# Zero products between the first transposes, other places for key transposes, query copies and weight splits in a two-layer trunk kernel

## The chip, the cores and the metric

The kernel runs on one core of a Trainium2 chip. A core has these engines: TensorE (PE, matrix products; PEld loads its stationary operand), VectorE (DVE), ScalarE (ACT), GpSimd (POOL), and SyncE (SP), on whose queue nearly all the transfers of this kernel stand. Each engine goes through its own instructions in the order in which the program issued them and waits on semaphores for the others. The metric is the time of one execution in microseconds (us); lower is better.

## What is computed

One inference step of a diffusion trunk: two layers over 1024 latent tokens (with 128 cached context keys) and 128 prompt tokens, model width 1024, all in float32. Cut to what matters here:

```python
for layer in range(2):
    mod = silu(c) @ w_mod[layer] + b_mod[layer]             # shift, scale, gate
    h = rms_norm(x, g_pre) * (1 + scale) + shift
    if layer == 0:                                           # A: attention, B: pooling
        q, k, v, ga, ub, gb = split(h @ w_in_e)
        q, k = axial_rope(rms_norm(q, q_norm)), axial_rope(rms_norm(k, k_norm))
        o_a = softmax(q @ [ctx_k, k].T / 8) @ [ctx_v, v]     # 8 heads on 2 key heads
        o_b = multiscale_pool(ub, b_map, b_scale)
        y = concat(o_a * silu(ga), o_b * silu(gb)) @ w_out_e
    else:                                                    # C: neighbourhood, D: latent attention
        y = concat(o_c * silu(gc), o_d * silu(gd)) @ w_out_o
    x = x + gate * rms_norm(y, g_post)
```

## The kernel before

Tokens lie in nine row tiles of 128 (eight latent, one prompt), the model width in eight slices k of 128. A float32 product is made of three: each operand is split into a high part, rounded to a type that PE takes at full rate, and a low part, the rest. So `hTh`/`hTl`, `whi`/`wlo`, `QP`, `KH`/`KL` are high and low halves: a high part is a cast, mostly on ACT, a low part a subtraction on DVE or POOL. `kn.vtt` is a two-operand instruction on DVE, `kn.ptt` the same on POOL, `kn.acopy` a copy or cast on ACT, `kn.tr` a transpose on PE through the identity.

The program is a list of stages. Within one, `weave(main, fill)` issues the main steps (products of PE) in order and puts the steps of `fill` between them by cost: every entry is (cost, function), and a fill step is issued when the costs before it have kept pace with those of the main list. `merge(a, b, off)` mixes two fill lists evenly. An entry whose function does nothing only spends cost, that is, pushes the next ones back. So the order on every engine is fixed when the program is built; an engine never goes past an instruction that waits.

What the change touches:

- **First stage** (lines 581 to 670): row tiles of x are loaded, normed and transposed in groups of three. `norm_x(t)` squares a tile with a row sum on ACT, takes the root and its reciprocal, and scales on DVE. `mod_block` makes the shift and scale columns that the norm of a slice needs; `pn(k, g)` transposes slice k of group g (`tp`), applies scale and shift (`hf`), casts `hTh` on ACT and makes `hTl` on POOL. `kvg` adds the products of key and value weights. `zeros(n)` issues n products of a zero tile into the same accumulators, which add nothing.
- **Query stage** (lines 803 to 814): `q_main(0)` and `q_main(1)` make the queries of four heads each. After every pair of row tiles `q_evac` norms and rotates it: a square on ACT, `hss`, `q` and the products `t` on DVE, `t` and `Q` on POOL. The keys come in the same way in pieces: `kv1` norms, `kv2` rotates (`t<-k,rtk` on DVE, `k` on POOL, `kp` for the prompt), and `kv3` transposes (`kT` on PE) and splits into `KH` (ACT) and `KL` (DVE). The argument 0 and 1 is the key tile of four row tiles each, 2 the prompt's. `wl` and `gs` are streams of weight chunks, `_load` issues the transfer, `need` the split.
- **Gate stage** (lines 925 to 942): twelve chunks `ch_main(0)` to `ch_main(11)` of gates and pooling input. In the last ones stand `units[0].prep` (the queries transposed and split, see below) and `maxima` of unit 0, with `rows` after the end of the stage.
- **Units 0 to 7**: attention of two heads and 512 queries each. `maxima` finds a row bound (`mp` products on PE, `mx` on DVE), `scores` makes `st` on PE and `P` on ACT, POOL adds the P of nine key tiles into `acc`, and `fin` divides the finished unit before: `divide` takes four reciprocals `srow` on DVE and then multiplies `oT` by `srow`. `split_heads` copies the transposed queries out of PSUM into `QP` (high part in its head's half, low part in the other) and `QM`.
- **Side work of the units**: `wo.split1(i, veng)` splits a slice of the output weights, the low part on DVE if the second argument is true, else on POOL.
- **Out projection of layer 0 and first chunks of layer 1** (lines 1364 to 1373): the stream `st` of layer 1's weight chunks; `fills[7]` and `fills[8]` are the fill lists of the last two row tiles. `H.make` norms the new x for layer 1 (`hf`, `hT1h`, and `hT1l` on POOL), `cg` are the first products of layer 1.
- **Latent attention of layer 1** (line 2260): `L.split_uk(1)`, one split of the key weights, in the side list of the units.

## Time and profile before

| | |
|---|---|
| median of three runs | 1590.68 us (1585.31 to 1592.05) |
| profiled execution, its own time | 1590.44 us |
| its span in the trace | 1588.6 us (1.84 us lie outside) |
| PE busy | 1517.0 us, 95% of the span |
| DVE, ACT, POOL busy | 803.0, 654.9, 613.6 us |

The stages lie in the span as follows: first stage and key and value projection to about 70 us, query stage to 142, gate stage to 320, units 0 to 7 to 540, out projection to 652, then layer 1 with the neighbourhood attention, the latent attention and its out projection.

A row of a timeline gives start, length, engine, line, operation and its tiles, the number of instructions that it joins, and in brackets how long the engine sat idle before it and which engine's work ended that. A matmul row shows 0.28 us for one product at full clock although they start 0.12 us apart: they are pipelined. [...]

### The profile page before, as it was taken

How to read it: one execution, taken by the hardware profiler on the slowest of the kernel's cores; microseconds unless marked ns; L12 is line 12 of the kernel's file. 1: busy time of each engine (PE TensorE's matmuls, PEld its weight loads, DVE VectorE, ACT ScalarE, POOL GpSimd, SP SyncE). 2: the span in 40 equal slices, each digit the busy share in tenths (PEclk: the TensorE clock that was granted, in tenths of full speed). 3: DMA queues.
4: the chain of work that ended last, by engine and by line, in shares of the span. 5: the costliest groups of instructions: out<-in, count | busy, mean ns of one | idle time of the engine just before them, and what ended most of it. 6: DMA issues, size and time to landing. Idle time of an engine off the chain costs nothing.

```text
span 1588.6 us, 23314 instructions
## 1 busy us (share of the span) xinstructions
PE 1517.0 (95%) x8927; PEld 1234.9 (78%) x8927; DVE 803.0 (51%) x1788; ACT 654.9 (41%) x1402; POOL 613.6 (39%) x508
## 2 busy tenths in 40 slices
PE   7989999989999999899999999999999999999998
PEld 5977999955555588798999999999976666665786
DVE  4574332347667655534354443424574545545643
ACT  4332222155554432435444544444454434445311
POOL 1643122057668423750312203101256656565221
PEclk8999999989999999999999999999999989999999
DMA  9334113130000222230403131131000000013241
GB/s 346 91 132 137 56 34 110 39 123 22 0 14 29 78 87 95 71 60 14 91 23 76 39 75 26 35 111 47 1 19 20 15 27 15 21 50 114 94 147 53
DMA packets 114078, 104.78 MB, mean 66 GB/s; under 512 B 41776, under 2 KB 99952, under 8 KB 113968
## 3 DMA queue, kind: packets, MB, share of 16 engines
q1 hardware_dynamic: 113792, 103.23, 21.6%
q8 instruction: 70, 1.15, 0.3%
q14 instruction: 40, 0.33, 0.1%
q10 hardware_dynamic: 176, 0.07, 0.0%
HBM read 87.54 MB, written 15.75 MB: 65 GB/s over the span
## 4 chain that ended last, share of the span: by engine, by line
PE 80%; DVE 8%; ACT 6%; POOL 3%; issue 2%; DMA 1%; SPq 0%; ACTq 0%; DVEq 0%; POOLq 0%
PE cg L115 15%; PE yps L115 11%; PE st L115 10%; PE gate L115 8%; PE pv L115 8%; PE lat L115 4%; PE mp L115 4%; PE cpv L115 3%; PE cS L115 2%; PE cT L124 2%; PE dq L115 2%; DVE mx L968 2%; PE qkv L115 1%; PE kv L115 1%; PE modps L115 1%
## 5 line engine op out<-in xcount | busy, mean ns | idle before, releaser
L968 DVE TENSOR_REDUCE mx<-mp 128x1 f32<-128x384 f32 x384 | 189.5, 547 | 99.9 <-PE mp L115 98.5
L142 POOL TENSOR_TENSOR acc<-acc,P 128x1024 f32<-128x1024 f32 x84 | 201.6, 2400 | 69.0 <-ACT P L1008 66.0
L1008 ACT ACTIVATE P<-st 128x512 f32<-128x512 f32 x256 | 148.4, 598 | 157.9 <-PE st L115 147.4
L115 PE MATMUL yps<-whi,ohl 128*128 128x512 f32 x576 | 182.8, 393 | 0.0
L115 PE MATMUL cg<-hT1h,whi 128*128 128x384 f32 x480 | 169.7, 353 | 1.8 <-DVE hf L151 1.2
L142 POOL TENSOR_TENSOR wlo<-raw,whi 128x1024 fp32r<-128x1024 f32 x30 | 72.0, 2401 | 247.5 <-ACT whi L131 172.3
L115 PE MATMUL cg<-hT1h,wlo 128*128 128x384 f32 x480 | 162.5, 339 | 1.9 <-POOL wlo L142 1.9
L115 PE MATMUL cg<-hT1l,whi 128*128 128x384 f32 x480 | 162.1, 338 | 0.0
L115 PEld LDWEIGHTS yps<-whi,ohl 128*128 128x128 f32 x576 | 108.1, 188 | 25.8 <-issue 3.7
L115 PE MATMUL yps<-wlo,ohl 128*128 128x512 f32 x288 | 112.1, 389 | 0.0
L115 PE MATMUL gate<-hTh,whi 128*128 128x384 f32 x288 | 99.2, 345 | 4.9 <-ACT whi L131 4.9
L115 PE MATMUL gate<-hTh,wlo 128*128 128x384 f32 x288 | 98.3, 341 | 0.3 <-DVE wlo L139 0.3
L115 PE MATMUL gate<-hTl,whi 128*128 128x384 f32 x288 | 97.8, 340 | 0.0
L115 PEld LDWEIGHTS cg<-hT1h,whi 128*128 128x128 f32 x480 | 90.7, 189 | 6.6 <-issue 3.3
L1616 ACT ACTIVATE cs<-cs,cnm 128x640 f32<-128x640 f32 (+1 forms) x64 | 54.8, 857 | 91.7 <-DVE cnm L149 91.1
L115 PEld LDWEIGHTS cg<-hT1h,wlo 128*128 128x128 f32 x480 | 90.6, 189 | 2.2 <-POOL wlo L142 2.2
L115 PEld LDWEIGHTS cg<-hT1l,whi 128*128 128x128 f32 x480 | 90.9, 189 | 0.5
L115 PE MATMUL pv<-P,dV 128*64 128x512 f32 x288 | 72.8, 633 | 1.7 <-DVE mx L968 1.7
L131 ACT CAST whi<-raw 128x1024 fp32r<-128x1024 f32 (+2 forms) x60 | 61.9, 1036 | 27.2 <-DMA raw<-in_w_in_e 12.8
L115 PE MATMUL mp<-KH,QP 128*128 128x384 f32 x192 | 61.3, 382 | 9.6 <-DVE QP L139 4.2
L139 DVE TENSOR_TENSOR wlo<-raw,whi 128x1024 fp32r<-128x1024 f32 (+2 forms) x30 | 38.4, 1288 | 61.4 <-ACT whi L131 56.0
L115 PE MATMUL st<-QH,dKh 96*128 96x512 f32 x144 | 63.5, 441 | 2.2 <-ACT P L1008 2.2
(424 smaller groups left out, 3563.8 us busy)
## 6 DMA issues: line engine op xcount, KB each, us to landing
raw<-in_w_in_o SPq DMA_DIRECT2D x20, 512.0 KB, 4.1
raw<-in_w_in_e SPq DMA_DIRECT2D x18, 512.0 KB, 7.5
wmb<-in_w_mod SPq DMA_DIRECT2D x16, 512.0 KB, 8.3
wm<-in_w_mod SPq DMA_DIRECT2D x16, 512.0 KB, 7.3
wg<-in_w_mod SPq DMA_DIRECT2D x16, 512.0 KB, 4.7
x<-xr SPq DMA_DIRECT2D x9, 512.0 KB, 4.8
xr<-x SPq DMA_DIRECT2D x9, 512.0 KB, 4.6
xn<-in_x_sample SPq DMA_DIRECT2D x8, 512.0 KB, 7.1
```

Source lines behind the costliest of these rows:

```text
L115: self.nc.tensor.matmul(out=out, lhsT=l, rhs=r, start=st, stop=sp)
L124: self.nc.tensor.transpose(out, in_, self.ident[0:n, 0:n])
L131: self.nc.scalar.copy(out=out, in_=in_)
L139: self.nc.vector.tensor_tensor(out=out, in0=a, in1=b, op=op)
L142: self.nc.gpsimd.tensor_tensor(out=out, in0=a, in1=b, op=op)
L968: kn.nc.vector.tensor_reduce(out=self.mx[:, h, t, c:c + 1], in_=b, axis=AX.X, op=ALU.max)
L1008: kn.nc.scalar.activation(out=P[:, h], in_=a, func=AF.Exp, scale=self.scale)
L1616: nc.scalar.activation(out=s[:, 0:n], in_=s[:, 0:n], func=AF.Exp, bias=nm, accum_out=sm)
```

## The change

1. First stage: `norm_x` of tiles 3 to 5 is split. The squares of tiles 3 and 4 (`norm_x1`) stand ahead of the first `pn`, that of tile 5 behind it; roots and scaling (`norm_x2`) follow. The six first transposes go in pairs with five zero products between; four stand before the mod block, ten instead of three behind it, and three each before, between and behind the next two `pn`. `kvg` issues its nine products by operand rather than by row tile.
2. Query stage: `kv3(0)` moves from `q_main(0)` to `q_main(1)`; there the order is `kv2(2)`, `kv2(1)`, `kv3(0)`, `kv3(2)`, `kv3(1)`, all ahead of the last six fill steps.
3. Gate stage: `units[0].prep` is in chunk 9, ten maxima pieces in chunk 10, the rest and the rows in chunk 11.
4. Units: the multiplication in `divide` is on POOL for five units; `split_heads` makes the low part before `QM`, and copies `QM` from `QP` in SBUF.
5. Weight splits: slice 5 of the output weights and the first four chunks of layer 1 have their low part on DVE; chunk 2 of the latter is loaded earlier and split in `fills[8]`; `split_uk(1)` is one slot earlier.

```diff
+    rx = {}
+    def norm_x1(t):
+        ss = rx[t] = kn.T([128, 1], tag="xss3", bufs=3)
+        nc.scalar.activation(out=kn.T([128, 1024], tag="sqx", bufs=1), in_=xn[t], func=AF.Square, accum_out=ss)
+    def norm_x2(t):
+        kn.vts(xn[t], xn[t], kn.rstd(rx[t], D, [128, 1], "x"))
...
     def kvg(k, ts):
-        for t in ts:
-            c = slice(128 * t, 128 * t + 128)
-            o = kvps(t)
-            kn.mm(o, hTh[k][:, c], kv.hi(k), False, False)
-            kn.mm(o, hTh[k][:, c], kv.lo(k), False, False)
-            kn.mm(o, hTl[k][:, c], kv.hi(k), False, k == 7 and (t == 8 or t % 2 == 1))
+        for i in range(3):
+            for t in ts:
+                c = slice(128 * t, 128 * t + 128)
+                last = i == 2 and k == 7 and (t == 8 or t % 2 == 1)
+                kn.mm(kvps(t), (hTl if i == 2 else hTh)[k][:, c], (kv.lo if i == 1 else kv.hi)(k), False, last)
...
     zeros(5, True, False)
-    tps = [kn.prenorm_t(k, xn[0:3]) for k in range(2)]
+    tps = [kn.B("tp") for k in range(2)]
+    for i in range(3):
+        for k in range(2):
+            kn.tr(tps[k][:, 128 * i:128 * i + 128], xn[i][:, 128 * k:128 * k + 128])
+        if i < 2:
+            zeros(5, False, False)
+    zeros(4, False, False)
     m = kn.mod_block(0, mb.pop(0))
     kn.mod_block_end(*m)
-    zeros(3, False, False)
+    zeros(10, False, False)
     kv.split1(0, True, 1)
+    for t in range(3, 5):
+        norm_x1(t)
     for k in range(2):
         pn(k, 0, tps[k])
+    norm_x1(5)
     kv.split1(0, True, 2)
     mb[2] = kn.mod_block_load(2)
     for t in range(3, 6):
-        norm_x(t)
+        norm_x2(t)
     for i in range(2):
         kvq(i)
+    zeros(3, False, False)
     for i in range(2, 4):
         pn(*seq[i])
+        zeros(3, False, False)
...
-            (500, lambda: None), (500, lambda: wl.need(1)), (1500, lambda: None), (500, lambda: kv3(0)), (1000, lambda: None)]
+            (500, lambda: None), (500, lambda: wl.need(1)), (3000, lambda: None)]
...
-    fill.insert(-5, (1, lambda: gs.need(0)))
-    fill = merge(fill, [(800, lambda: kv2(2)), (500, lambda: kv3(2)), (800, lambda: kv2(1)), (500, lambda: None), (500, lambda: kv3(1))], 1)
+    fill.insert(-6, (1, lambda: gs.need(0)))
+    kvs = [(800, lambda: kv2(2)), (800, lambda: kv2(1)), (500, lambda: kv3(0)), (500, lambda: kv3(2)), (500, lambda: kv3(1))]
+    fill = merge(fill[:-6], kvs, 1) + fill[-6:]
     weave(q_main(1), fill, 0.9)
...
+        if i == 9:
+            fill += units[0].prep(kn.W)
         if i == 10:
-            fill += units[0].prep(kn.W)
+            f, rows = units[0].maxima()
+            fill += f[:10]
         if i == 11:
-            f, rows = units[0].maxima()
-            fill += f
+            fill += f[10:] + rows
         weave(ch_main(i, evac), fill, 0.9)
     p2.__exit__(None, None, None)
-    for _, f in rows:
-        f()
...
-def divide(kn, b, g, parts=4):
+def divide(kn, b, g, parts=4, tt=None):
...
-            kn.vtt(g(), g(), box["r"])
+            (tt or kn.vtt)(g(), g(), box["r"])
...
     for h in range(2):
-        kn.acopy(QM[h], b[rs[h]])
+        kn.vtt(QP[h][rs[1 - h]], b[rs[h]], f32(QP[h][rs[h]]), ALU.subtract)
     for h in range(2):
-        kn.vtt(QP[h][rs[1 - h]], b[rs[h]], f32(QP[h][rs[h]]), ALU.subtract)
+        kn.acopy(QM[h], f32(QP[h][rs[h]]))
...
-        L = divide(kn, lambda: self.sb, self.gT, 4 if self.p < 3 else 2)
+        L = divide(kn, lambda: self.sb, self.gT, 4 if self.p < 3 else 2) if 2 * self.p + self.hf > 4 else divide(kn, lambda: self.sb, self.gT, 4, kn.ptt)
...
-        side.setdefault((u, kt + 3), []).append((1, lambda i=i: wo.split1(i, i > 5)))
+        side.setdefault((u, kt + 3), []).append((1, lambda i=i: wo.split1(i, i > 4)))
...
-    st = Stream([Chunk(kn, w_in[:, c:c + 128], 128, alloc="s" if i > 16 else "w") for i, c in enumerate(cols)])
+    st = Stream([Chunk(kn, w_in[:, c:c + 128], 128, alloc="s" if i > 16 else "w", veng=i < 4) for i, c in enumerate(cols)])
...
-    fills[8].insert(12, (1, lambda: st._load(2)))
+    fills[8].insert(4, (1, lambda: st._load(2)))
+    fills[8].append((1, lambda: st.need(2)))
...
-    side, extra = {(0, 1): post0}, {7: [(18000, lambda: None)] + pre}
+    side, extra = {(0, 0): [(1, lambda: L.split_uk(1))], (0, 1): post0}, {7: [(18000, lambda: None)] + pre}
```

On PE in the first stage, from the zero products at the start to behind the first mod block (`modps` from `wmb` is the mod block, from `mrow` and `brow` its transposes; - is the order before, + the order now):

```order
 L115 MATMUL kv<-zero 128x512 x11
-L124 MATMUL tp<-ident,xn 128x128 x6
+L124 MATMUL tp<-ident,xn 128x128 x2
+L115 MATMUL kv<-zero 128x512 x5
+L124 MATMUL tp<-ident,xn 128x128 x2
+L115 MATMUL kv<-zero 128x512 x5
+L124 MATMUL tp<-ident,xn 128x128 x2
+L115 MATMUL kv<-zero 128x512 x4
 L115 MATMUL modps<-wmb,silrep 32x128 x32
 L124 MATMUL modps<-ident,mrow 128x128
 L124 MATMUL modps<-ident,brow 128x48
+L115 MATMUL kv<-zero 128x512 x10
```

The six transposes, in one row before, are three pairs with zero products behind each.

On DVE in the query stage, behind the scaled queries of the first pair of `q_main(1)` (`t<-k,rtk` belongs to key tile 1, `KL` of 64x512 to key tile 0, `KL` of 64x128 and `KLp` to the context and prompt keys):

```order
 L139 TENSOR_TENSOR q<-qkv,hr 128x512
-L139 TENSOR_TENSOR t_1392<-q,rtq 128x8x16 x4
-L139 TENSOR_TENSOR KLp<-kT,KHp 64x128 x2
-L139 TENSOR_TENSOR KL_895<-kT,KH_893 64x128
-L139 TENSOR_TENSOR KL_896<-kT,KH_894 64x128
+L139 TENSOR_TENSOR t_1411<-q,rtq 128x8x16 x4
+L139 TENSOR_TENSOR t_1434<-k,rtk 128x4x16 x8
+L139 TENSOR_TENSOR KL_925<-kT,KH_923 64x512
+L139 TENSOR_TENSOR KL_926<-kT,KH_924 64x512
 L544 TENSOR_REDUCE hss<-sq 128x8
```

The key products of tile 1 and the two `KL` of tile 0 came in between the first and the second pair, and the small ones went further back.

On POOL in one unit, from its first sum to the memset for the next maxima, before:

```order
L142 TENSOR_TENSOR acc<-P 128x1024
L142 TENSOR_TENSOR acc<-acc,P 128x1024 x2
L142 TENSOR_TENSOR acc<-acc,Px 128x1024 x2
L142 TENSOR_TENSOR wlo<-raw,whi 128x1024
L142 TENSOR_TENSOR acc<-acc,P 128x1024 x3
L972 MEMSET ms 128x194
```

and now, with the product of `oT` of the unit before:

```order
L142 TENSOR_TENSOR acc<-P 128x1024
L142 TENSOR_TENSOR acc<-acc,P 128x1024 x2
L142 TENSOR_TENSOR acc<-acc,Px 128x1024 x2
L142 TENSOR_TENSOR wlo<-raw,whi 128x1024
L142 TENSOR_TENSOR acc<-acc,P 128x1024 x2
L142 TENSOR_TENSOR oT_2654<-oT_2654,srow 128x512
L142 TENSOR_TENSOR acc<-acc,P 128x1024
L993 MEMSET ms 128x194
```

The product came in ahead of the last sum of the unit.

## Rows read from the trace of the kernel before

**Rows 1.** The page: busy time, share of the span, instructions of each engine.

```profile
PE 1517.0 (95%) x8927; PEld 1234.9 (78%) x8927; DVE 803.0 (51%) x1788; ACT 654.9 (41%) x1402; POOL 613.6 (39%) x508
```

**Rows 2.** The chain of the first 50 us: start, length, engine, tile, line, count.

```profile
14.07 3.04 PE modps L115 x64
...
23.34 1.14 ACT sqx L337 x2
...
44.91 1.88 PE modps L115 x64
```

**Rows 3.** Windows: length, busy PE, PEld, DVE, ACT, POOL, then PEclk, DMA, GB/s.

```profile
13.00:16.00 3.00, 3.00 (x44) 2.52 (x48) 0.00 (x0) 1.04 (x1) 0.00 (x0) 0.50 1.08 385
113.00:119.00 6.00, 4.53 (x25) 3.36 (x29) 3.86 (x11) 1.86 (x7) 4.11 (x7) 0.72 0.44 146
326.00:330.00 4.00, 4.00 (x12) 3.61 (x12) 3.49 (x8) 1.19 (x2) 0.00 (x0) 0.50 0.70 273
416.00:428.00 12.00, 10.24 (x34) 4.96 (x33) 6.52 (x12) 3.65 (x7) 4.05 (x2) 0.72 0.00 1
664.00:668.00 4.00, 2.77 (x9) 2.77 (x10) 3.58 (x5) 2.30 (x8) 3.94 (x3) 0.60 0.00 0
```

**Rows 4.** Timeline of ACT, first stage.

```profile
19.59 1.10 ACT L131 CAST hTh<-hf 128x384 fp32r<-128x384 f32 x2 [3.66 <-DVE hf L151]
```

**Rows 5.** Timeline of PE, first stage, the zero products behind the mod block.

```profile
17.92 0.97 PE L115 MATMUL kv<-zero 128*128 128x512 f32 x3
```

**Rows 6.** Timeline of PE, query stage and second gate chunk.

```profile
94.78 1.11 PE L124 MATMUL kT<-ident,k 128*128 128x128 f32 x4 [2.90 <-POOL k L142]
...
109.96 0.28 PE L115 MATMUL qkv<-wlo,hTh 128*128 128x256 f32 x1
110.08 0.28 PE L115 MATMUL qkv<-whi,hTl 128*128 128x256 f32 x1
114.47 0.44 PE L124 MATMUL kT<-ident,kp 128*128 128x128 f32 x2 [4.12 <-POOL kp L142]
...
159.87 0.69 PE L115 MATMUL gate<-hTh,whi 128*128 128x384 f32 x1 [4.90 <-ACT whi L131]
```

**Rows 7.** Timeline of DVE, query stage.

```profile
91.06 2.26 DVE L139 TENSOR_TENSOR t<-k,rtk 128x64 f32<-128x64 f32 x8 [1.64 <-POOL Q L142]
...
104.23 1.38 DVE L139 TENSOR_TENSOR KL<-kT,KH 64x512 fp32r<-64x512 f32 x2
107.47 0.69 DVE L544 TENSOR_REDUCE hss<-sq 128x8 f32<-128x512 f32 x1 [1.86 <-ACT sq L542]
...
139.53 1.39 DVE L139 TENSOR_TENSOR KL<-kT,KH 64x512 fp32r<-64x512 f32 x2 [2.41 <-ACT KH L131]
142.78 0.69 DVE L544 TENSOR_REDUCE hss<-sq 128x8 f32<-128x512 f32 x1 [1.86 <-ACT sq L542]
```

**Rows 8.** Timeline of POOL, query stage.

```profile
93.47 1.26 POOL L142 TENSOR_TENSOR k<-t,t 128x512 f32<-128x512 f32 x1 [1.17 <-DVE t L139]
...
117.36 1.41 POOL L142 TENSOR_TENSOR Q<-t,t 128x256 f32<-128x256 f32 x2 [0.92 <-DVE t L139]
```

**Rows 9.** Timeline of ACT at the end of the gate stage.

```profile
320.03 1.49 ACT L131 CAST QM<-mT 1x256 fp32r<-1x256 f32 x4
```

**Rows 10.** Timeline of DVE at the end of the gate stage.

```profile
323.93 1.41 DVE L139 TENSOR_TENSOR QP<-qT,QP 64x512 fp32r<-64x512 f32 x2 [5.14 <-ACT QM L131]
```

**Rows 11.** Timeline of PE: gate stage's end, prompt in the units, layer 1's first chunks.

```profile
324.67 1.65 PE L115 MATMUL mp<-KH,QP 128*128 128x384 f32 x4 [2.60 <-DVE QP L139]
...
419.19 1.19 PE L115 MATMUL mp<-KH,QP 128*128 128x384 f32 x2 [1.56 <-DVE QPp L139]
...
665.23 0.69 PE L115 MATMUL cg<-hT1h,wlo 128*128 128x384 f32 x1 [1.87 <-POOL wlo L142]
```

**Rows 12.** One tile (oT), 320 to 545 us: duration in ns, min/median/max.

```profile
L139 DVE TENSOR_TENSOR oT<-oT,srow x7: 693/1146/2579, 379.1 to 540.7; 128x512 f32<-128x512 f32 x7
```

**Rows 13.** Timeline of POOL, a unit's first sum and the idle time before it.

```profile
387.17 2.38 POOL L142 TENSOR_TENSOR acc<-P 128x1024 f32<-128x1024 f32 x1 [2.03 <-ACT P L1008]
```

More of the change, by code (lines that the diff above doesn't have):

```diff
@@ L2260, in layer1_latent @@
     pre0 = VA[:2] + VA[4:]
-    post0 = [(330, lambda: L.kstep(0, 1152, 128)), (1, lambda: L.split_uk(1))]
+    post0 = [(330, lambda: L.kstep(0, 1152, 128))]
     ak = [(1, lambda i=i: L.alloc_K1(i)) for i in range(5)]
```

## The prediction

> **What bounds the kernel now.** I read the page's busy times first: PE is busy 1517.0 us of a span of 1588.6, the other engines about half of it or less [rows 1]. So the end is set by PE's work, by the clock at which it runs, and by what little PE waits. [...] I therefore went through PE's waits in order of time and set the granted clock of a window beside each one [rows 3]. A window of length w at mean clock c holds at most w x (1 - c) of clock loss; I call that its clock loss.
>
> The sum is made against the profiled run's own 1590.44 us (the span and 1.84 around it). The median of the runs, 1590.68, is 0.24 away, which changes nothing here.
>
> **First stage.** Three edits work together. (a) The mod block takes 3.04 us at 14.07, and the same 64 products take 1.88 at 44.91 [rows 2]; the granted clock of 13 to 16 us is 0.50 [rows 3]. Zero products now fill the waits between the transposes ahead of it. If they hold the full clock, 3.04 - 1.88 = 1.16 us goes. (b) ACT stands idle 3.66 us until hf comes, casts hTh at 19.59 [rows 4], and only then squares x of the next three row tiles, 1.14 us for one with its accumulator read [rows 2]. Two of the three squares now stand ahead of the casts, in that idle time: 2 x 1.14 = 2.3 us leaves the way to the next transposes. (c) The new products of zeros are 5 + 5 + 4 + 7 + 3 + 3 + 3 = 30. Three took 0.97 us [rows 5], so some 0.3 each and 9 us in all. They cost nothing while PE waits anyway: the present three end at 18.9, and hTh's casts only start at 19.59 [rows 4, 5]. But those waits shrink by what (b) wins, and a zero that is still queued when data comes delays PE. I take 1.16 + 2.3 = 3.5 us. Bounds: 5 if the second mod block also comes to the full clock (the same 1.16, and a little), and -2 if some 7 of the 30 overrun.
>
> **Query stage.** In the first half PE waits 2.90 us for the key sum k and 4.12 for kp, and at the start of the second gate chunk 4.90 for a weight cast [rows 6]. The window of 113 to 119 has clock 0.72 [rows 3], so 6 x 0.28 = 1.7 us of clock loss goes with such a wait. The four transposes kT of key tile 0, with its 4 ACT casts and the two KL on DVE (1.38 us together [rows 7]), and the transposes of kp go to the second half. Both waits go with them: 2.90 + 4.12 + 2 x 1.7 = 10.4 us if nothing came in their place.
>
> Something does. DVE's 8 products of key tile 1 (2.26 us in the row of tile 0 [rows 7]) and POOL's sum of them (1.26) now stand behind the first query pair of the second half. POOL finished that pair at 117.36 + 1.41 = 118.8 [rows 8]. That comes earlier by the KL pair that left and by the DVE wait behind it, 1.38 + 1.86 = 3.2 us [rows 7], so at 115.6; 2.26 on DVE and 1.26 on POOL then give 119.1 for kT of tile 1. Where is PE by then? It came to kp's transposes at 114.47 - 4.12 = 110.35; without the first stall that is 110.35 - 2.90 - 1.7 = 105.8. Ahead of these transposes there are now 72 more query products at 0.12 us apart [rows 6]: 8.6 us, so 114.4. A **new wait of 119.1 - 114.4, about 5 us**, with its 1.7 of clock loss, takes the place of the two, and PE by itself would win 10.4 - 6.7 = 3.7. The other engines agree: DVE's last whole pairs waited 2.41 for KH and 1.86 for sq [rows 7], and with KL of tile 1 done before them both go, 4.3 us. With them POOL's last instruction of the stage comes earlier; SP issues the next stage's loads, the second gate chunk's weights among them, only behind it. So that chunk moves with this chain, and its wait of 4.90 stays. I take 4.1, between the two. Bounds: 2 (casts of tiles 0 and 1 delay the query pairs between them) and 9 (the new wait doesn't form).
>
> **End of the gate stage.** Unit 0's copies of q come one chunk earlier, and the rows of its maxima inside the last chunk. Before, ACT copied the rows after the gate's end (1.49 us [rows 9]) and then QP and QM; DVE waited 5.14 us for QM before QP's low half [rows 10], and PE 2.60 for that [rows 11]. The 1.49 now lies beside gate products and QM no longer stands before DVE, so PE's 2.60 goes nearly whole. The next limit is the exponentials, which ACT reaches 1.49 earlier and no more, since QM still stands ahead of them. That gives 1.5, and of the clock loss of 326 to 330, 4 x 0.50 = 2.0 us [rows 3], I take 1.5: 3.0 us. Bounds 1 and 4.6 (2.60 + 2.0).
>
> **Units 0 to 7.** QM is copied from SBUF behind the casts while DVE makes the low half at once. At the prompt's part PE waits 1.56 us for QPp [rows 11], and 12 x 0.28 = 3.4 us of clock loss lies in that window [rows 3]. I take 1.6 + 2.4 = 4.0. Bounds: 0 if DVE is late for another reason, 8 if other units win as much. In the same units the product of oT and srow goes from DVE to POOL, five times. On DVE it took between 0.69 and 2.58 us [rows 12]. On POOL I take 1.3, by its sum of the same 128x512 shape, 1.26 [rows 8]. DVE is not the bound, so nothing is counted for it. On POOL the idle time at a unit's end, 2.03 us [rows 13], covers the 1.3; if it doesn't, see rival 3.
>
> What made DVE's time vary from 0.69 to 2.58 [rows 12] is work beside it. [...]
>
> **Layer 1's first chunks.** The low parts of the first four weight chunks go from POOL to DVE, and the third chunk's load and split come earlier. PE waits 1.87 us for POOL's wlo at 665.23 [rows 11], and 4 x 0.40 = 1.6 us of clock loss goes with it [rows 3]: 3.5 us. Bounds 1 (DVE's splits and POOL's hT1l slow each other) and 6 (shorter waits before it go too).
>
> **The rest.** One split of the output weights goes from POOL to DVE where neither holds PE up, and a split of layer 1's key weights comes one slot earlier, where PE has no wait. Their cover is PE's products of the units; both count as nothing, and without cover each costs its own length, some 1.3 us by POOL's sum above.
>
> **Sum:** 3.5 + 4.1 + 3.0 + 4.0 + 3.5 = 18.1, so 1590.4 - 18.1 = **1572.3 us**. The bounds add to -2 + 2 + 1 + 0 + 1 = 2 and 5 + 9 + 4.6 + 8 + 6 = 32.6: 1588 and 1558.
>
> **Rivals.**
> 1. **The new key wait doesn't form.** The query stage then gives 9 to 10.4 and not 4.1, and the time is 1566. For it: PE's place is counted, not read. Against it: nothing on DVE ahead of those products goes but what I took off. Chance 0.15.
> 2. **Only the bare waits go, and the clock falls as often as before.** The zeros overrun or don't hold the clock, and the waits that are left lie elsewhere with the same half clock behind them. Then 1 us is won in the first stage, 2 in the query stage, 1.5 at the gate's end, 1.6 in the units, 1.9 in layer 1: 8 in all, 1582. For it: half of my sum is clock loss, and every stage keeps some wait. Against it: the waits of the last three stages get no successor that I can find. Chance 0.22.
> 3. **POOL becomes the bound of the units, and the kernel gets slower.** The product stands in POOL's queue ahead of the unit's last sum of acc, and srow has one buffer, so DVE's next reciprocal waits for POOL, and the maxima behind it on DVE too. If it takes 2.58 us as on DVE at worst [rows 12], it is longer than the idle 2.03 [rows 13]; five units then lose the 2.58 each and a clock loss like the 3.4 of 416 to 428 [rows 3]: 5 x 6 = 30, against 14.1 won elsewhere: 1606. It decides from 2.03 us on. Against it: alone on its engine it took 0.69. Chance 0.07.
>
> The forecast has the remaining 0.56.
>
> **How the numbers follow.** A difference of 0.5%, 8 us, is about what a measurement of this kernel can tell from no change. The forecast's own spread is 1564 to 1580, faster by over 8 us in nearly all of it (0.53 of 0.56); rival 1 is faster (0.15); rival 2 lies on the border at 1582, half on each side (0.11 and 0.11); of rival 3 0.05 is slower by over 0.5%, the rest within. So faster 0.79, same 0.16, slower 0.05. The range holds the forecast, rival 1 and most of rival 2, and leaves out rival 3 and the corners of the bounds: 1561 to 1587.
>
> **What would show it.** In the trace after: a first mod block of 1.9 us, and the second three transposes some 3.5 us earlier; one wait for kT of about 5 us, 115 to 119 less the first stage's gain, and no other in the query stage; the second gate chunk at about 159.9 - 3.5 - 4.1 = 152.3, still behind a wait near 5; no wait of mp at the gate's end, none for QPp, none for wlo in layer 1's first chunks. I am wrong if those waits are gone and the span is no shorter (then the clock fell elsewhere), or if POOL shows no idle time at the units' ends (rival 3).

## The result, and the profile after

The changed kernel takes 1570.36 us in the median of four runs (1566.6 to 1571.76), against 1588.88 for the kernel before in its own four (1585.31 to 1592.05): a ratio of 0.988, 95% interval 0.985 to 0.991. Two later comparisons of the same two kernels gave 0.987 (0.985 to 0.989) and 0.988 (0.986 to 0.990). The profiled run took 1571.76 us, 18.7 less than the profiled run of before; 18.1 were forecast.

The page's first part, and two of the longest rows of its fifth, of the changed kernel:

```profile
PE 1510.9 (96%) x8957; PEld 1231.8 (78%) x8957; DVE 803.6 (51%) x1788; ACT 655.4 (42%) x1402; POOL 606.6 (39%) x508
...
L115 PE MATMUL cg<-hT1h,whi 128*128 128x384 f32 x480 | 169.2, 352 | 0.3 <-DVE hf L151 0.3
L115 PE MATMUL cg<-hT1h,wlo 128*128 128x384 f32 x480 | 161.9, 337 | 0.0
```

PE has 30 instructions more than before (the zeros) and is busy for 6.1 us less [rows 1]: the products are the same, they ran at a higher mean clock (0.984 granted over the span, 0.978 before). The rest of the span, in which PE is idle, fell from 71.6 to 59.1 us. The wait of `cg` for wlo is gone.

The total says little about the parts. For those I read where each stage's first product starts (the view of one tile gives the first and the last start) and set PE's idle time and the clock loss of every stage beside it, the latter from windows of 1 us. The stages are cut at the first product of the next; the gates end with the start of their last product, the latent units go from their first score to the start of their last pv. Two traces of the kernel before and three of the changed kernel, all in us; "loss" is length times (1 - granted clock), as in the prediction. The granted clock is the share of full speed that the profile gives; in the first trace of each kernel its record holds 1.00 and 0.50 alone, so a value between is the mean of a window with both:

| stage | before: length (idle, loss) | before, 2nd trace | after | after, 2nd | after, 3rd | won, forecast |
|---|---|---|---|---|---|---|
| first stage | 70.4 (11.1, 5.1) | 70.5 (11.1, 5.1) | 68.3 (8.4, 0) | 67.8 (8.3, 0) | 68.1 (8.0, 0) | 3.5 |
| queries | 71.7 (7.2, 3.4) | 71.7 (7.2, 3.4) | 67.9 (4.9, 1.7) | 67.8 (4.8, 1.7) | 67.9 (4.6, 1.7) | 4.1 |
| gates | 177.0 (6.1, 3.4) | 175.3 (5.8, 1.7) | 175.1 (4.9, 3.4) | 175.7 (5.0, 3.4) | 174.2 (5.0, 1.7) | 0 |
| gates' end to first pv | 17.0 (3.9, 3.4) | 16.4 (3.9, 1.7) | 13.9 (1.9, 1.7) | 13.8 (1.9, 1.7) | 13.7 (1.9, 0) | 3.0 |
| units 0 to 7 | 206.6 (10.3, 6.8) | 206.6 (10.7, 5.1) | 197.0 (7.7, 1.7) | 197.1 (7.7, 1.7) | 195.5 (7.6, 0) | 4.0 |
| out projection | 110.8 | 110.8 | 110.8 | 110.8 | 110.8 | 0 |
| layer 1 to first cS | 58.6 (2.5, 1.7) | 57.4 (2.5, 0) | 55.2 (0.7, 0) | 55.1 (0.7, 0) | 55.2 (0.7, 0) | 3.5 |
| neighbourhood attention | 357.0 (7.2, 0) | 356.9 (7.2, 0) | 358.7 (7.7, 1.7) | 358.8 (7.7, 1.7) | 358.8 (7.7, 1.7) | 0 |
| latent units | 316.2 (14.5, 10.2) | 313.9 (15.1, 6.8) | 319.4 (14.6, 13.6) | 316.3 (14.5, 10.2) | 313.9 (15.1, 6.8) | 0 |
| span | 1588.6 | 1582.8 | 1570.0 | 1566.9 | 1561.8 | 18.1 |

(The latent preparation, 96.1 to 96.5, and the last out projection, 107.2, are left out.) At the start of layer 1's `cS` the first trace of the changed kernel is 23.9 us ahead; at the end it is 18.6 ahead. So the sum came out right with terms that didn't: the units won more than twice their forecast, the first stage less, and layer 1 took back 5.

The waits, from PE's timeline of the changed kernel in five stretches (start, length, engine, line, operation, idle before and its releaser):

```profile
14.18 1.95 PE L115 MATMUL modps<-wmb,silrep 128*32 128x128 f32 x64
...
32.76 0.33 PE L124 MATMUL modps<-ident,mrow 128*128 128x128 f32 x1 [1.83 <-DVE mrow L136]
...
96.48 0.44 PE L115 MATMUL qkv<-wlo,hTh 128*128 128x256 f32 x1 [1.99 <-DVE wlo L139]
...
118.36 0.63 PE L124 MATMUL kT<-ident,k 128*128 128x128 f32 x4 [2.03 <-issue]
...
152.56 0.69 PE L115 MATMUL gate<-hTh,whi 128*128 128x384 f32 x1 [3.68 <-ACT whi L131]
...
314.42 1.08 PE L115 MATMUL mp<-KH,QP 128*128 128x384 f32 x4 [1.86 <-DVE QP L139]
...
403.72 0.94 PE L115 MATMUL mp<-KH,QP 128*128 128x384 f32 x2 [0.56 <-DVE QPp L139]
```

The first mod block has full speed (1.95 in this view, near the 1.88 of [rows 2]). Behind the second one stands a wait that before was half a microsecond: 1.83 for mrow. In the query stage the waits of 2.90 and 4.12 [rows 6] became two of 1.99 and 2.03. The second gate chunk starts at 152.56 (152.3 forecast), the waits for QP and QPp are 1.86 and 0.56 in place of 2.60 and 1.56 [rows 11]. The prediction had both as gone.

### The profile page after: what moved, and what is told of

The parts are those of the page before. It is cut to its first block, busy times and chain, and to the rows that moved or that the text cites. A ratio compares the mean times of both kernels' runs of the same rounds, so it can differ in the third digit from the quotient of the medians.

```text
span 1570.0 us, 23369 instructions
## 1 busy us (share of the span) xinstructions
PE 1510.9 (96%) x8957; PEld 1231.8 (78%) x8957; DVE 803.6 (51%) x1788; ACT 655.4 (42%) x1402; POOL 606.6 (39%) x508
## 4 chain that ended last, share of the span: by engine, by line
PE 81%; DVE 9%; ACT 5%; DMA 2%; issue 2%; POOL 1%; SPq 0%; DVEq 0%; ACTq 0%; POOLq 0%
PE cg L115 14%; PE yps L115 12%; PE st L115 10%; PE gate L115 9%; PE pv L115 9%; PE lat L115 4%; PE mp L115 4%; PE cpv L115 3%; PE cS L115 2%; PE cT L124 2%; PE dq L115 2%; DVE mx L989 2%; DMA raw<-in_w_in_e 1%; PE kv L115 1%; PE dv L115 1%
## 5 line engine op out<-in xcount | busy, mean ns | idle before, releaser
L142 POOL TENSOR_TENSOR acc<-acc,P 128x1024 f32<-128x1024 f32 x84 | 200.6, 2388 | 67.4 <-ACT P L1029 64.5
L142 POOL TENSOR_TENSOR wlo<-raw,whi 128x1024 fp32r<-128x1024 f32 x25 | 60.0, 2400 | 245.8 <-ACT whi L131 174.4
L139 DVE TENSOR_TENSOR wlo<-raw,whi 128x1024 fp32r<-128x1024 f32 (+2 forms) x35 | 46.6, 1340 | 65.3 <-ACT whi L131 64.6
```

The source lines that it names most:

```text
L139: self.nc.vector.tensor_tensor(out=out, in0=a, in1=b, op=op)
L142: self.nc.gpsimd.tensor_tensor(out=out, in0=a, in1=b, op=op)
```

## The experiments

Theory: the parts are separate, and each wins its stage's waits and the clock's falls beside them. Rivals: the loads of x, not the zeros, set the end of the first stage; DVE's chain, not PE's waits, sets the query stage; in the units the product on POOL did more than the order of the copies; and layer 1 gives time back because of the change, or only because the clock falls at other moments. Each kernel below is the changed one with the edit shown; lengths come from one trace each, so the clock's falls are set beside them.

### The two kernels again

> The kernel before once more, for its trace. In the first trace its granted clock falls in sixteen places inside the span, each with a clock loss of 1.7 or 3.4 us, 34 in all. If the falls belong to the waits of the program, all sixteen stand again in the same places with the same sizes. If chance has a part, some of those in layer 1 (1269 to 1443 us) change between 0, 1.7 and 3.4 while the waits beside them stay, and the time moves by as much: 1585 to 1594.

> The changed kernel once more. Its first trace is ahead of before by 24 us at 690 us of the span and by 18.7 at the end; layer 1 gives 5 us back in three places where the same waits stand but the clock fell where it hadn't, or for twice as long. If that is placement of the clock's falls by chance, this trace has another loss there (0 to 7) with the same waits. If the change does it, the same three places lose again. Time 1566 to 1572.

> The changed kernel a third time, beside the one above on the same chip. Up to 1143 us of the span the same as in the two traces of it within 0.6 us; from there to the last pv, 313 to 320 us, by where the clock falls, with the same waits of 14.5 us in sum. Time 1566 to 1572.

`rep_before` took 1584.54 us in its one run, `rep_after` 1568.09 and `rep_after2` 1570.0 in the median; their stages stand in the table. The lengths up to the units repeat within 0.6 us where the clock loss is the same. Of the sixteen falls of the clock in the first trace of before the second has twelve, and what differs lies in the gates, their end and the units as well as in layer 1. The latent units' length doesn't repeat: 319.4, 316.3 and 313.9 for one kernel, 316.2 and 313.9 for the other. Here is one place in them, as windows (time, length, busy time and instructions of PE, PEld, DVE, ACT, POOL, granted clock, DMA share, GB/s), of the changed kernel's first trace:

```profile
1143.40:1462.80 319.40, 304.84 (x1434) 200.80 (x1432) 171.31 (x310) 150.13 (x289) 189.02 (x112) 0.96 0.13 39
1346.00:1353.00 7.00, 7.00 (x21) 4.33 (x22) 1.83 (x7) 4.56 (x9) 5.25 (x3) 0.52 0.13 37
```

and of its second:

```profile
1143.40:1459.70 316.30, 301.79 (x1435) 199.32 (x1433) 171.21 (x309) 149.95 (x289) 188.98 (x112) 0.97 0.13 40
1346.00:1353.00 7.00, 7.00 (x26) 4.14 (x26) 1.83 (x7) 4.56 (x9) 5.25 (x3) 0.76 0.24 73
```

The stage starts at 1143.4 in both, PE is idle for 14.6 and 14.5 us, DVE, ACT and POOL do the same in the same 7 us; the clock was 0.52 in one and 0.76 in the other, and PE issued 21 products against 26. The transfers differ too, 37 against 73 GB/s; which follows from which, the rows don't tell. So the latent units' part of what layer 1 gave back (3.2 us) is not the change's: the same program has it or doesn't. The neighbourhood attention's 1.7 is another matter: it stands in all three traces of the changed kernel, behind a wait of 1.37 us for cQP that was 0.98 before, and in neither trace of before. The edited kernels below show how far that goes.

### First stage

`undo_first` has the first stage of before, with its `kvg`, in short:

```diff
-    for t in range(3, 5):
-        norm_x1(t)
     for k in range(2):
         pn(k, 0, tps[k])
-    norm_x1(5)
...
     for t in range(3, 6):
-        norm_x2(t)
+        norm_x(t)
```

with the zeros as before too. `no_zeros` keeps the early squares and the new `kvg`, without the added zeros:

```diff
-        if i < 2:
-            zeros(5, False, False)
-    zeros(4, False, False)
...
-    zeros(10, False, False)
+    zeros(3, False, False)
...
-    zeros(3, False, False)
     for i in range(2, 4):
         pn(*seq[i])
-        zeros(3, False, False)
```

> The changed kernel with the first stage of before. Measured for this part so far: the first query product comes at 68.3 us and not at 70.4. If the parts add, it comes at 70.4 here, and everything behind it 2.1 later. If the loads of x set the end of this stage, a part of the 2.1 stays.

> The changed kernel without the 30 added zero products, the squares and the operand order as changed. If the zeros hold the clock, as forecast, the first mod block goes from 1.95 us to about 3.0 and the clock falls in the places of before (13 to 16, 23 to 26, 30 to 33); the first query product comes at 69.3 to 70 us. If the squares alone make the gain, the mod block is slow but the query products still start at 68.3, since the loads of x (the last squares wait for them until 27.3) set the end.

`undo_first`: the first query product comes at 70.0 us, the later stages are those of the changed kernel (67.9, 175.3, 13.8, 197.1): the parts add. Its run still took 1567.87 us, no more than the changed kernel's, as its latent units happened to take 313.4; a part of 2 us is seen in a stage, not in the end.

`no_zeros`: 68.8, between the two. Its first mod block and two windows, from PE's timeline and the windows view:

```profile
13.56 3.22 PE L115 MATMUL modps<-wmb,silrep 128*32 128x128 f32 x64
```

```profile
13.00:16.00 3.00, 3.00 (x50) 2.50 (x54) 0.00 (x0) 0.42 (x1) 0.00 (x0) 0.50 1.08 382
20.00:23.00 3.00, 2.83 (x11) 2.40 (x12) 2.28 (x3) 2.15 (x6) 2.85 (x2) 0.50 1.09 349
```

and the first of these windows in the changed kernel:

```profile
13.00:16.00 3.00, 3.00 (x71) 2.42 (x69) 0.00 (x0) 0.60 (x1) 0.00 (x0) 1.00 1.07 380
```

So the zeros do hold the clock: without them the stage has 5.1 us of clock loss and 11.3 of idle time, with them 0 and about 8.3. What they win of the stage's length is another question. The second mod block and the wait behind it, from PE's timeline of the kernel before:

```profile
31.66 2.74 PE L115 MATMUL modps<-wmb,silrep 128*32 128x128 f32 x64
34.84 0.33 PE L124 MATMUL modps<-ident,mrow 128*128 128x128 f32 x1 [0.45 <-DVE mrow L136]
```

of `no_zeros`:

```profile
29.74 1.95 PE L115 MATMUL modps<-wmb,silrep 128*32 128x128 f32 x64
33.67 0.33 PE L124 MATMUL modps<-ident,mrow 128*128 128x128 f32 x1 [1.97 <-DVE mrow L136]
```

and of the changed kernel:

```profile
28.97 1.95 PE L115 MATMUL modps<-wmb,silrep 128*32 128x128 f32 x64
```

The block ends at 30.9 us in the changed kernel, 3.5 earlier than before, and without the zeros at 31.7, still 2.7 earlier. Then PE waits for mrow either way, 1.83 and 1.97 us. What it waits for is in the chain of the changed kernel's first 50 us (start, length, what):

```profile
17.30 9.98 DMA xn<-in_x_sample
27.30 1.16 ACT sqx L337 x2
...
31.75 0.75 DVE xn L149
32.50 0.21 DVE mrow L136
32.76 0.34 PE modps L124
```

The first square of the third group starts at 27.30, when its tile of x has landed and ACT's casts of hTh are done, both within 0.1 us of it (27.28 and 27.23). DVE scales that group until 32.5, and mrow, ready when the second mod block ends at 30.9, stands behind it on DVE. Before, the same block ended at 34.4 and nothing was in its way. ACT's row of that square, in the kernel before and in `no_zeros`:

```profile
28.14 1.05 ACT L337 ACTIVATE sqx<-xn 128x1024 f32<-128x1024 f32 x1
...
28.22 1.06 ACT L337 ACTIVATE sqx<-xn 128x1024 f32<-128x1024 f32 x1 [0.60 <-DMA xn<-in_x_sample]
```

From the start of this square to mrow's transpose it is 5.45 us in `no_zeros` and in the changed kernel alike, and from there some 35 to the first query product. In the trace of `no_zeros` x landed 0.9 us later. So the 0.5 us by which its stage is longer can be that load's alone, and the zeros' own gain in this stage is not shown; in the eight traces with the changed first stage the first query product comes at 67.7 to 68.6. The squares and the operand order, which were not tried apart, make 1.2 to 1.7 us at least.

### Query stage

`undo_q` has the fills of before in `q_main(0)` and `q_main(1)`:

```diff
-    fill.insert(-6, (1, lambda: gs.need(0)))
-    kvs = [(800, lambda: kv2(2)), (800, lambda: kv2(1)), (500, lambda: kv3(0)), (500, lambda: kv3(2)), (500, lambda: kv3(1))]
-    fill = merge(fill[:-6], kvs, 1) + fill[-6:]
+    fill.insert(-5, (1, lambda: gs.need(0)))
+    fill = merge(fill, [(800, lambda: kv2(2)), (500, lambda: kv3(2)), (800, lambda: kv2(1)), (500, lambda: None), (500, lambda: kv3(1))], 1)
```

> The changed kernel with the query stage of before. From the first query product to the first gate product: 71.7 us before, 67.9 after, 3.8 won (forecast 4.1). Here 71.7 again, with kT waits of 2.9 and 4.1. The second gate chunk then waits 4.9 and not 3.7; if its load and the chain on DVE and POOL move together, as forecast, the last gate product is 5 us later than in the changed kernel (3.8 + 1.2).

The stage takes 71.5 us (71.7 expected), and the last gate product comes 5.3 us later after its start than in the changed kernel (71.5 + 176.8 against 67.9 + 175.1; 5.0 expected). The kT waits are 2.88 and 3.02. So this part wins 3.6 to 3.8 us in its stage and 1.1 to 1.7 in the gate stage behind it, where the wait at the second chunk is 3.68 and not 4.90.

`mend` splits the second query weight before the keys' products; `mend2` gives that split to POOL instead. Both also move the third group's scaling in the first stage:

```diff
-    for t in range(6, 9):
-        norm_x(t)
+    for t in range(6, 9):
+        norm_x1(t)
...
-    for i in range(4, 7):
+    for i in range(4, 6):
         pn(*seq[i])
+    for t in range(6, 9):
+        norm_x2(t)
+    pn(*seq[6])
...
-    fill = [(1, lambda: kv1(0)), ... (800, lambda: kv2(0)), (500, lambda: None), (500, lambda: wl.need(1)),
+    fill = [(1, lambda: kv1(0)), ... (500, lambda: wl.need(1)), (800, lambda: kv2(0)), (500, lambda: None),
```

> The changed kernel with two further edits. (1) First stage: the changed kernel's second mod block ends at 30.9 us, but DVE copies mrow only at 32.4, behind the scaling of the third group of x, whose loads land at 27.3; here that scaling stands behind the hf of the first two slices. If that wait of 1.83 us is on the path, the first query product comes 1 to 1.8 us earlier than 68.3; if the rest of the stage is bound elsewhere, it doesn't move. (2) Query stage: the changed kernel waits 1.99 us for wlo at 96.5, with a fall of the clock; here the split stands ahead of the key products. If PE is the bound there, 3.7 us go; if DVE's chain up to key tile 1 is, the wait for that tile's kT (2.03) grows by as much, and from the first query product to the first gate product it takes 67 to 68 us as now. Time 1563 to 1571.

```diff
+        sd[t] = kn.T([128, 1], tag="xsd3", bufs=3)
+        nc.scalar.activation(out=sd[t], in_=rx[t], func=AF.Sqrt, scale=1.0 / D, bias=kn.eps[0:128])
...
     for i in range(4, 7):
         pn(*seq[i])
+    for t in range(6, 9):
+        r = kn.T([128, 1], tag="xr3", bufs=3)
+        nc.vector.reciprocal(out=r, in_=sd[t])
+        kn.vts(xn[t], xn[t], r)
...
-    wl = Stream([Chunk(kn, w_in[:, 0:256], 256, veng=True), Chunk(kn, w_in[:, 256:512], 256, veng=True)])
+    wl = Stream([Chunk(kn, w_in[:, 0:256], 256, veng=True), Chunk(kn, w_in[:, 256:512], 256)])
...
-    fill = [(1, lambda: kv1(0)), (500, lambda: kv1(2)),
+    fill = [(1, lambda: kv1(0)), (1, lambda: wl.need(1)), (500, lambda: kv1(2)),
```

> The changed kernel with two other edits, each for what the first try of this kind left open. (1) Query stage: with wlo of the second query chunk moved ahead on DVE, the wait for kT of key tile 1 was 5.4 us and the stage as long as before (68.4 us). So DVE's chain up to that key tile is the bound by one theory: then the two splits on POOL, which is idle from 78 to 87 us there, take 2.9 us off DVE's chain, the wait for kT falls to 2.5 or less with no wait for wlo, and the stage takes 64 to 66 us. By the other theory the bound is the load of the second gate chunk, and the first gate product comes earlier but that chunk's wait grows by as much: gate stage 177 to 178. (2) First stage: the roots of the third group stand right behind its squares on ACT, and its scaling on DVE behind the hf of the first three pieces. If mrow's wait of 1.83 us is what bounds the stage, the first query product comes 1 to 1.8 us ahead of the changed kernel's; if the scaling is then late for the third group's transposes, no gain. Time 1562 to 1570.

Medians 1569.7 (ratio 0.988, 0.986 to 0.991) and 1567.1 (0.986, 0.984 to 0.988): neither can be told from the changed kernel. In the first stage both lost, 70.2 and 71.4 us to the first query product. mrow's wait fell from 1.83 to 0.44, but the third group's transposes then wait for its scaling, three waits of 0.4 to 1.0 us with a fall of the clock behind them (a loss of 1.7 us in `mend`, 3.4 in `mend2`). The wait for mrow and this one are the two ends of the same DVE work.

In the query stage the wait for wlo went, and the one for kT of tile 1 took its place; PE's timeline of `mend` and of `mend2` there:

```profile
120.10 1.09 PE L124 MATMUL kT<-ident,k 128*128 128x128 f32 x4 [5.40 <-issue]
```

```profile
120.37 1.08 PE L124 MATMUL kT<-ident,k 128*128 128x128 f32 x4 [4.78 <-issue]
```

From the stage's first product to this transpose it is 50.1 us in the changed kernel (118.36 - 68.3), 49.9 in `mend` and 49.0 in `mend2`. PE's waits ahead of it can be moved, but this point hardly moves with them. The stage takes 68.4 us in `mend` and 67.4 in `mend2`, where 64 to 66 were expected if DVE's chain sets it: 2.9 us of splits taken off DVE brought only 1, and DVE waits 2.51 for sq there, behind ACT's casts for these splits. The load of the second gate chunk, the other theory, is out: the gate stage takes 174.6 us in `mend2` and not 177 to 178.

What ends the wait for kT the rows don't name ("issue"). Two rows of the changed kernel lie close to it, one of POOL and one of ACT:

```profile
115.89 1.27 POOL L142 TENSOR_TENSOR k<-t,t 128x512 f32<-128x512 f32 x1 [1.17 <-DVE t L139]
...
117.09 1.17 ACT L131 CAST KH<-kT 64x512 fp32r<-64x512 f32 x2 [7.36 <-DVE KL L139]
```

The key sum k is done at 117.16, but PE starts at 118.36, 0.1 us behind the last casts KH of key tile 0. In the two other traces of the changed kernel, in `mend` and in `mend2` PE also starts 0.1 us behind these casts and 1.2 behind k. So the casts and `KL` of tile 0, which the change put beside tile 1, look like the end of the chain; no run has them elsewhere, so this is read from the rows and not tested.

### Gates' end and units

`undo_gate` puts unit 0's copies and rows back, `undo_heads` the order of QM and the low half, `undo_pool` the product of oT and srow; the three edits in this order:

```diff
-        if i == 9:
-            fill += units[0].prep(kn.W)
         if i == 10:
-            f, rows = units[0].maxima()
-            fill += f[:10]
+            fill += units[0].prep(kn.W)
         if i == 11:
-            fill += f[10:] + rows
+            f, rows = units[0].maxima()
+            fill += f
...
+    for _, f in rows:
+        f()
```

```diff
-    for h in range(2):
-        kn.vtt(QP[h][rs[1 - h]], b[rs[h]], f32(QP[h][rs[h]]), ALU.subtract)
-    for h in range(2):
-        kn.acopy(QM[h], f32(QP[h][rs[h]]))
+    for h in range(2):
+        kn.acopy(QM[h], b[rs[h]])
+    for h in range(2):
+        kn.vtt(QP[h][rs[1 - h]], b[rs[h]], f32(QP[h][rs[h]]), ALU.subtract)
```

```diff
-        L = divide(...) if 2 * self.p + self.hf > 4 else divide(kn, lambda: self.sb, self.gT, 4, kn.ptt)
+        L = divide(kn, lambda: self.sb, self.gT, 4 if self.p < 3 else 2)
```

> The changed kernel with unit 0's copies and rows at the places of before, but the new order of QM and the low half. From the last gate product to the first pv: 17.0 us before, 13.9 after. If the place of the rows made the gain (1.49 of ACT), it comes to 15.5 or more here; if the order of QM did, it stays at 14.

> The changed kernel with QM copied from PSUM again ahead of DVE's low half. The forecast gives the whole gain of the units to this order: then the stretch from the first pv to the out projection comes back to 202 to 206.6, with the waits of mp for QP (0.5 to 0.6) and for QPp (1.6) and the clock's falls behind them. If most of the 9.6 is DVE's free time, it stays below 200. The gate stage's end loses too: 1 to 2 us.

> The changed kernel with the product of oT and srow back on DVE in all units. Units from the first pv to the first product of the out projection: 206.6 us before, 197.0 after, so 9.6 won where 4.0 were forecast (all of it for the order of QM and the low half). If the product on POOL has nothing in it, as forecast, this stretch stays at 197. If DVE's 0.7 to 2.6 us for it held PE up, it comes to 199 to 202, with more waits of mp and sum for DVE.

Medians: `undo_heads` 1577.16 (0.993, 0.991 to 0.995), `undo_pool` 1565.26 (0.986, 0.983 to 0.990); `undo_gate` 1570.9 in one run. The gates' end takes 15.3 us in `undo_gate` and 16.0 in `undo_heads`, against 13.9: the place of the rows is worth 1.4 us, the order of QM 2.1, before was 17.0. (`undo_heads` also copies QM from PSUM again; order and source were not tried apart.) PE had two waits here before, the second of them in [rows 11]; the first:

```profile
321.57 0.50 PE L115 MATMUL st<-QM,KL 65*128 65x512 f32 x1 [1.30 <-ACT QM L131]
```

In `undo_gate` it is back, and the wait for QP is 1.43:

```profile
312.71 0.50 PE L115 MATMUL st<-QM,KL 65*128 65x512 f32 x1 [1.30 <-ACT QM L131]
314.64 1.65 PE L115 MATMUL mp<-KH,QP 128*128 128x384 f32 x4 [1.43 <-DVE QP L139]
```

In `undo_heads` it stays away, and the wait for QP is 3.02:

```profile
315.27 1.65 PE L115 MATMUL mp<-KH,QP 128*128 128x384 f32 x4 [3.02 <-DVE QP L139]
```

So the place of the rows takes away the wait of 1.30, and the order of QM 1.2 us of the wait for QP.

The units from the first pv on, as one window each. `undo_heads`:

```profile
326.90:533.60 206.70, 196.40 (x864) 106.92 (x864) 138.53 (x229) 114.08 (x207) 151.41 (x73) 0.97 0.07 24
```

`undo_pool`:

```profile
324.30:524.50 200.20, 192.55 (x864) 106.49 (x863) 148.50 (x234) 115.22 (x207) 146.49 (x67) 0.97 0.08 24
```

The changed kernel:

```profile
325.20:522.20 197.00, 189.33 (x865) 105.20 (x864) 140.31 (x229) 115.16 (x207) 150.90 (x72) 0.99 0.08 25
```

With the old order all 9.6 us are gone again, and PE's idle time is 10.3 as before. With the product on DVE, DVE is busy for 8.2 us more and POOL for 4.4 less, and PE's idle time is the same 7.6: the product's place changes no wait of PE. The 3.2 us by which `undo_pool` is longer here are clock loss, 5.1 against 1.7. Whether they come with the product on DVE one trace can't tell: in the ten traces that have it on POOL and the new order of QM the loss of this stage is 0 or 1.7, so 5.1 is outside what the table shows of chance. Against it, this was the slowest of four executions, and the others took 7 to 10 us less. So `undo_pool` with its lower median is no better kernel that I could show, nor a worse one; the intervals overlap.

### Layer 1's first chunks

`undo_l1` has the stream `st` and the fill of before:

```diff
-    ... alloc="s" if i > 16 else "w", veng=i < 4) for i, c in enumerate(cols)])
+    ... alloc="s" if i > 16 else "w") for i, c in enumerate(cols)])
...
-    fills[8].insert(4, (1, lambda: st._load(2)))
-    fills[8].append((1, lambda: st.need(2)))
+    fills[8].insert(12, (1, lambda: st._load(2)))
```

> The changed kernel with layer 1's first weight chunks as before (low parts on POOL, the third loaded later). From the first cg product to the first cS: 58.6 us before, 55.2 after (forecast 3.5 won). Here 58.6 again, with the wait of 1.9 for wlo and one fall of the clock (1.7 us). If the wait had gone for another reason, less.

57.3 us against 55.2; PE's timeline there:

```profile
642.93 0.44 PE L115 MATMUL cg<-hT1h,whi 128*128 128x384 f32 x1 [0.63 <-ACT whi L131]
645.41 0.44 PE L115 MATMUL cg<-hT1h,wlo 128*128 128x384 f32 x1 [1.86 <-POOL wlo L142]
```

The wait is back, and the clock stayed full this time (the row at 645.41 is 0.44 long, not the 0.69 of [rows 11]). So 2.1 us are the wait's, and 1.2 to 1.3 more in a trace in which the clock falls behind it. The neighbourhood attention is back at 357.0 here, without its clock loss of 1.7. It is also without that loss in `undo_heads`, `undo_pool`, `undo_gate`, `mend` and `mend2`, which have this part of the change, and it has the loss in `undo_first`, `no_zeros` and `undo_q`. The wait for cQP takes one of two lengths, 1.37 to 1.39 us in seven of the fourteen traces and 0.98 to 1.02 in the other seven; the clock falls behind the long one in five, behind the short one in one. No single edit goes with either length. What sets it, no run shows.

## Why the prediction was right, point by point

- **What bounds it.** PE's waits and the clock beside them: held. Idle time fell by 12.5 us and the clock loss by 10 from the first trace of before to the first after, by 13.6 and 4 between the second ones: the waits' half of the sum is firm, the clock's half changes with the execution. No other engine became the bound.
- **First stage, 3.5 forecast, 2.1 to 2.7 measured.** The mod block's clock did what the text says, and at the end of the second mod block PE is ahead by the 3.5 us of the forecast. The step that failed is the sum of the two terms as if both lay on the path to the stage's end: mrow queues on DVE behind the third group of x, which the prediction doesn't mention, and that group's chain starts only 0.8 us earlier than before (28.14 to 27.30). 1.4 us go in that wait. A sign of the prediction failed with it: of the second three transposes the one that waits for xn starts at 24.53, before at 25.84, so 1.3 us earlier and not 3.5. The 30 zeros didn't overrun; that they win a part of the stage isn't shown.
- **Query stage, 4.1 forecast, 3.8 measured.** Nearly right in size, wrong in two details of its path. PE is held 2.0 at wlo ahead of kT of tile 1, a split that stood behind the old kT wait and so showed no wait in the trace of before; "no other" wait was wrong, and `mend` has the wait of 5 (5.40) with wlo out of the way. And the sum k was ready when the text says (48.9 us behind the stage's first product, 119.1 - 70.4 = 48.7 in the forecast), but PE starts 1.2 us later, with the end of the casts of key tile 0, which the sum has as moved and not as a limit.
- **Second gate chunk.** Its start agreed (152.3 and 152.56), partly by luck: the two stages ahead of it won 5.9 us in the first trace and not 7.6, and its wait is 3.68, not 4.90. The gate stage's length moved from 177.0 and 175.3 to 174.2 to 175.7, about 1 us on the mean, which wasn't forecast.
- **Gates' end, 3.0 forecast, 3.1 measured** in the first pair of traces, 2.6 in the second. The two causes held, the rows' place and the order of QM, but the path did not. PE's wait for QP was to go "nearly whole"; 1.86 of 2.60 is left. In its place the wait of 1.30 for the copied rows went, which the prediction doesn't name. Nor are the exponentials the next limit: PE's idle time there is 1.9 us, and the wait for QP is all of it.
- **Units, 4.0 forecast, 9.6 measured.** The mechanism was right (`undo_heads`), the term mis-sized; 9.6 lies even above its bound of 8. I priced one wait, the prompt's, and part of the clock behind it. The order of QM acts in every unit: PE's idle time fell by 2.6 us, of which 1.0 was at the prompt, and the clock loss by 5.1, from three falls to one. 1.9 us remain that stand in no row of idle time. What DVE's time for the product of oT and srow goes with, the trace of before shows: six of the seven in [rows 12] lie beside a sum of acc on POOL, take 1.15 to 2.58 us and end 0.55 us behind that sum; the seventh, with POOL idle, takes 0.69. That the product on POOL changes no wait of PE, as forecast, `undo_pool` shows; its part in the clock loss is open. Rival 3 is out: POOL took the five products in 1.27 to 1.30 us each (1.3 forecast), and PE had no wait for it.
- **Layer 1's first chunks, 3.5 forecast, 3.4 measured** in the first pair of traces; 2.1 of it without a fall of the clock. The lower bound of 1 has DVE's splits and POOL's hT1l slow each other, which no run shows: in the first trace of the changed kernel the four splits take 1.22 to 1.23 us each, and hT1l takes 1.00 to 1.03 (630 to 680 us; the same before, 640 to 680). A cast of cKH on POOL is longer beside the fourth split, 1.53 us against 0.50 before; PE is idle for 0.7 us in the whole stage.
- **What wasn't in the sum.** Layer 1 lost 5.3 us behind that point in the first trace (1.7 + 0.4 + 3.2). The 3.2 are chance, as the second and third trace show (316.3, 313.9); the 1.7 come in all three traces of the changed kernel, but in only three of the nine edited ones.
- **The rivals.** Rival 1 (no new key wait): the wait was shorter, but only because another came ahead of it. Rival 2 (bare waits only) said that the clock falls as often: before layer 1's latent part it falls in eleven places before (23.8 us of loss; nine in the second trace), in five after (10.2, with the neighbourhood attention's; five and three in the others). It is out for that part. The latent units, where the change takes no wait, lose as much as before, 6.8 to 13.6 us.
- **The small edits.** The out projection takes 110.8 us in every trace, so the split moved to DVE costs and wins nothing there. The split of layer 1's key weights moves (`post0` no longer has it, a line that the diff at the start leaves out) and wasn't tried alone; PE's idle time in the latent units is the same to 0.1 us in the first pair.

So the total agreed by 0.6 us by luck: +5.6 in the units and about +1.9 in the gate stage stand against -1.4 in the first stage and -5.3 in layer 1. The forecast was right in that waits of PE and the clock behind them go, and where; three of its five terms (queries, gates' end, layer 1's first chunks) were right in size.

## What to carry to other kernels

Judge a change of many parts by the lengths of its stages and by PE's idle time in them, and set the clock loss of each stage beside it: what an edit wins in idle time repeats to 0.1 to 0.6 us in most stages here (not in the first two, where traces of the same code had 6.7 to 8.5 and 4.6 to 6.1), what it wins in clock changes from one execution to the next by more than the smaller edits are worth (the latent units of one kernel lost 13.6, 10.2 and 6.8 us in three traces). When a wait is removed, look not only at what is late next but at what was issued behind the old wait and never had to wait itself (wlo here, mrow in the first stage, and perhaps the casts of key tile 0). An edit in a routine that every unit calls should be priced at each of its calls, the short waits too.

## What the runs showed of the hardware

In the fourteen traces nearly every fall of the granted clock has a loss of 1.7 us or of twice that, 3.4, whatever wait stands before it: 1.7 behind the 5.40 of `mend`, 3.4 behind the 1.30 below. In the first trace of each kernel a fall is a stretch of 3.41 or 6.83 us at 0.50. The clock also falls behind waits shorter than those of the sum: in the latent units of the changed kernel there is a fall behind the first of these rows,

```profile
1246.39 0.41 PE L115 MATMUL mp<-dKh,QH 96*128 96x384 f32 x1 [1.30 <-DVE dKl L139]
...
1343.82 0.44 PE L115 MATMUL dpvp<-dPp,dVp 128*64 128x128 f32 x4 [0.82 <-ACT psum L131]
1344.79 0.41 PE L115 MATMUL mp<-dKh,QH 96*128 96x384 f32 x1 [0.53 <-DVE dKl L139]
```

and one behind the other two, where waits of 0.82 and 0.53 follow each other; each of the two falls has a loss of 3.4. The same wait has a fall of 1.7 in one execution and 3.4 in the next, with DVE, ACT and POOL in step (1346 to 1353 above: a clock of 0.76 against 0.52 in the same 7 us).

With products of zeros ahead of the first mod block the clock was full there, without them half: 1.00 in the changed kernel, 0.50 in `no_zeros` and before, in the same 3 us of the first stage (13 to 16).

PE takes rounded operands faster than plain float32: in the trace of before a product of 128x256 takes 0.28 us with rounded ones (`qkv`, median) and 0.38 with plain ones (`ggp`).
